# Cross attention of a decoder step: three heads' softmax ahead of the sample rows', outputs and sample sums in the order of their operands, other PSUM banks

## The chip, the cores and the metric

The kernel runs on one core of a Trainium2 chip. The metric is the device time in microseconds (us). Before the change it was 1386.8 us, the median of three runs (1386.02 to 1387.09). An engine's instructions run in an order that is fixed when the program is built; engines wait for one another by semaphores. TensorE (PE) writes its results to eight PSUM banks, ScalarE (ACT) and VectorE (DVE) read them from there.

## The reference

One decoder layer is computed for 256 prompt rows and 8 sample rows, 264 in all, with a model width of 2048. The part that matters here is the cross attention into 256 memory tokens, with four heads of width 128. The prompt rows attend to keys and values computed from the memory; the sample rows attend to keys and values from a cache, a set of their own for each of the 8 rows.

```python
def memory_kv(mem, g_mem, w_ck, w_cv, ck_norm_g):
    h = rms_norm(mem, g_mem)
    k = rms_norm((h @ w_ck).reshape(b, m, MEM_HEADS, MEM_HEAD_DIM), ck_norm_g)
    v = (h @ w_cv).reshape(b, m, MEM_HEADS, MEM_HEAD_DIM)
...
def cross_attend(x, mem_k, mem_v, g_cross, w_cq, cq_norm_g, w_co):
    q = rms_norm((rms_norm(x, g_cross) @ w_cq).reshape(b, t, MEM_HEADS, MEM_HEAD_DIM), cq_norm_g)
    logits = jnp.einsum('bqhd,bshd->bhqs', q, mem_k.astype(q.dtype), ...) * MEM_HEAD_DIM ** -0.5
    p = jax.nn.softmax(logits, axis=-1)
    o = jnp.einsum('bhqs,bshd->bqhd', p.astype(x.dtype), mem_v.astype(x.dtype))
    return o.reshape(b, t, D_XATTN) @ w_co
```

Ahead of it stand an attention and a state-space mixer with their output projection (`w_out`); behind it a feed-forward block (`w_up`, a convolution, a gate, `w_down`).

## The kernel before

The whole layer is one stream of matmuls. Activations lie with features in the partitions and the 264 rows in the free dimension. Every weight is loaded in parts of 128 x 1024 (`weights`, L76), cast to a high part on ScalarE (L89) and a low part on DVE (L90), and each product is three matmuls: high x high, high x low, low x high (`mm3`, L103 to L106). `proj` (L108) runs a projection with its results in PSUM banks and hands them to an evacuation function. The small matrix work, such as logits, transposes and sums, is in full fp32.

PSUM has eight banks, named by tags (L59): `mm` has three, `t` two, and `s`, `x` and `y` one each. A tile of a tag waits until the former tile of the same slot has been read for the last time, in the order in which the program asks for them. So two pieces of work with the same tag cannot overlap where there is one bank.

The order of each engine's instructions is not the program's. A scheduler runs the program in a simulation when it is built: at each step it takes the ready instruction that stands first in the program, and lays down the engine's order that comes out. Program order is thus a priority. `tc.high_priority()` puts instructions ahead (the weight casts and evacuations); `tc.issue_after(x)` makes the instructions of a block stand behind x on x's engine. On the chip the laid-down order stays, whatever the real durations are.

The cross attention runs through these steps. `keys` (L1105) computes the memory keys `kx`. `q_pair` (L1070) computes the queries of two heads; `q_rms` (L1081) their norms `fq`. Then, in program order:

- `sample_probs` (L1134): the sample rows' logits against the cached keys, in two halves of four rows each (L1144, bank `x`), as the `kt` buffers allow; the sum of squares of the sample queries (L1154, bank `y`); the root and its reciprocal (L1158, recorded under the helper's lines L287 and L288); the maximum (L1160); the exponentials (L1163); the normalization (L1165); the transposes (L1168, recorded under L283; bank `t`) and the copies into `pz` (L1172).
- `probs(h, f)` for the four heads (L1194): logits of the prompt rows in bank `s` (L1198), maximum (L1201), two exponentials (L1206), reciprocal and scaling (L1207, L1209), four transposes (L1213, recorded under L283; bank `t`) and a copy into `pts` on ScalarE (L1214). The exponentials lie in a buffer `e` of which there are two.
- `v_pair(0)` (L1217): the memory values of heads 0 and 1 in two of the three banks `mm`, read out by ScalarE (L1230).
- `sample_out` (L1174): the sample rows' output against the cached values (L1180, bank `x`), four steps on DVE that gather each head's columns into `rs` (L1183, L1185), a transpose (L1188, recorded under L283; bank `y`), and the split of the sample columns into high and low parts `OH` and `OL` (recorded under L97).
- `out_head(0)` and `out_head(1)` (L1232): the output of a head for the prompt rows (L1236), in bank `y` for even and `s` for odd heads, and its split (L97).
- `v_pair(1)`, `out_head(2)` and `out_head(3)`.
- the output projection `w_co` (L1289 to L1304) with the residual in `x2_ev` (L1285). Its first weight unit runs through the four heads in turn and needs each head's `OH` and `OL` with the sample columns. The other three stand behind the split of the last head on ScalarE and DVE.

Then the feed-forward block begins: `up(0)` (L1361) takes two banks for each pair of weight units, `mm` for even and `t` for odd ones (L1374). Its results stay in the banks until `r2`, the norm of the rows, is known.

Of the kernel before, what the change touches and what calls it, by code (L numbers as in the profile page):

```python
# [9 lines left out]
AF = mybir.ActivationFunctionType  # L10
ALU = mybir.AluOpType
# [37 lines left out]
def hybrid_decoder_step_kernel(ctx: ExitStack, tc: tile.TileContext, I, O):  # L49
    nc = tc.nc  # L50
    V, S, P, PE = nc.vector, nc.scalar, nc.gpsimd, nc.tensor
# [9 lines left out]
    def psum(tag):  # L61
        return ps.tile([128, 512], F32, tag=tag, name=tag, bufs=banks[tag])
# [38 lines left out]
    marks = {}  # L101
# [47 lines left out]
    op = oc.enter_context(tc.tile_pool(name="op", bufs=1))  # L149
# [135 lines left out]
    def rms(out, ss, n):  # L285

        S.activation(out=out, in_=ss, func=AF.Sqrt, bias=eps[0:out.shape[0]], scale=1.0 / n)  # L287
        V.reciprocal(out=out, in_=out)  # L288
# [141 lines left out]
    p = psum("y")  # L430
# [40 lines left out]
    p = psum("x")  # L471
# [661 lines left out]

    def sample_probs():  # L1134
        lg = psum("x")
        for half in range(2):
            kts = []
            for b in range(4):
                kts.append(wide("kt")[:, 0:1024].rearrange("p (m s) -> p m s", m=4))
                nc.sync.dma_start(out=kts[b], in_=I["mk"][4 * half + b])  # L1140

            def logits(b, m):
                c = 128 * (4 * half + b) + 32 * m
                return PE.matmul(lg[32 * m:32 * m + 32, 0:256], qz[:, c:c + 32], kts[b][:, m, :],  # L1144
                                 start=half == 0 and b == 3, stop=half == 1 and b == 2)

            with tc.issue_after(marks["q"].ins):
                marks["q"] = logits(3, 0)
            with tc.issue_after(marks["q"].ins):
                for b in (3, 0, 1, 2):  # L1150
                    for m in range(b == 3, 4):
                        logits(b, m)
        p = psum("y")
        PE.matmul(p[:, 0:1], qq.rearrange("p m b -> p (m b)"), ones[:, 0:1], start=True, stop=True)  # L1154
        st = xp.tile([128, 4], F32, name="sst")
        fs, mx, den = st[:, 0:1], st[:, 1:2], st[:, 2:3]
        V.tensor_tensor(out=fs, in0=p[:, 0:1], in1=r1s[:, 1:2], op=ALU.mult)
        rms(fs, fs, 128)  # L1158
        V.tensor_tensor(out=fs, in0=fs, in1=r1s[:, 0:1], op=ALU.mult)
        V.tensor_reduce(out=mx, in_=lg[:, 0:256], op=ALU.max, axis=AX.X)  # L1160
# [13 lines left out]
    def sample_out():  # L1174
# [9 lines left out]
        for m in range(1, 4):  # L1184
            V.scalar_tensor_tensor(out=rs, in0=po[:, m * 128:m * 128 + 128], scalar=cst[:, C_M4 + m:C_M4 + m + 1], in1=rs,  # L1185
                                   op0=ALU.mult, op1=ALU.add)
        p = psum("y")
        tr(p[:, 0:128], rs)  # L1188
# [5 lines left out]
    def probs(h, f):  # L1194
        p = psum("s")
        s3 = p.rearrange("p (c k) -> p c k", c=2)
# [7 lines left out]
        e3 = e.rearrange("p (c k) -> p c k", c=2)  # L1204
        for c in range(2):
            S.activation(out=e3[:, c, :], in_=s3[:, c, :], func=AF.Exp, scale=f[:, c:c + 1], bias=mx[:, c:c + 1], accum_out=den[:, c:c + 1])  # L1206
        V.reciprocal(out=den, in_=den)  # L1207
# [55 lines left out]
    OH, OL = OHL[:, 0:4, :], OHL[:, 4:8, :]  # L1263
    sample_probs()
    for b in range(6, 8):
        vts.append(wide("vt")[:, 0:1024].rearrange("p (k n) -> p k n", k=2))
        nc.sync.dma_start(out=vts[b], in_=I["mv"][b])
    for h in range(2):
        probs(h, fq[:, :, h])
    for h in range(2, 4):  # L1270
        probs(h, fq[:, :, h])
    for i in range(2):
        v_pair(i)
        if i == 0:
            sample_out()
        for m in range(2):
            heads = out_head(2 * i + m)
    nc.sync.dma_start(out=O["mem_v"], in_=vx)
# [82 lines left out]
    def up(g):  # L1361
        H = (rows("A", f"hh{g}"), rows("A", f"hl{g}"))
        n = len(groups[g])
        for ii, i in enumerate(groups[g]):
# [8 lines left out]

            proj([w_up[2 * i], w_up[2 * i + 1]], X2, ev, tag="t" if i % 2 else "mm")  # L1374
            cs = []
# [213 lines left out]
```

## Time and profile before

| | |
|---|---|
| Median of three runs | 1386.8 us (1386.02 to 1387.09) |
| The profiled execution | 1386.54 us |
| Its span, first to last instruction | 1384.3 us |
| Granted TensorE clock | 1.000 |
| DVE busy | 1048.7 us (76%) |
| ScalarE busy | 766.1 us (55%) |
| GpSimd busy | 94.8 us (7%) |
| HBM traffic | 215 GB/s over the span |

The profile is of one execution. Its span is 2.2 us less than that execution's own time. Times of single instructions are in microseconds from the span's start; the cross attention's part after the queries lies between 554 and 620. A row of the timeline gives start, duration, engine, line, operation, what is written and read, the shape, how many instructions were merged in the row, and in brackets how long the engine stood idle before it and what ended that. PE's matmuls overlap, so their durations are longer than the distance from one start to the next. A full fp32 matmul has two records. In the row of a window each engine's busy time is given with the number of its instructions; PEld is the loading of weights into PE.

### The profile page before, as it was taken

The numbers are of one execution on the slowest core, as the hardware profiler recorded it, in microseconds if no ns is written. First come the engines' busy times: TensorE is split into PE (matmuls) and PEld (weight loads), VectorE is DVE, ScalarE is ACT, GpSimd is POOL, SyncE is SP. The second block draws the span as 40 slices with busy tenths as digits, with TensorE's granted clock in tenths as the row PEclk, the third lists the DMA queues.
The fourth block names the chain that finished last, engine by engine and source line by source line (L and its number), as shares of the span: only waits on it lengthen the run. The fifth ranks groups of instructions, "written<-read, shape, count | busy, mean of one in ns | idle before, by whom it ended". The sixth has DMA issues, their size and how long they took to land.

```text
span 1384.3 us, 28768 instructions
## 1 busy us (share of the span) xinstructions
PE 1376.5 (99%) x11415; PEld 1348.3 (97%) x11415; DVE 1048.7 (76%) x1865; ACT 766.1 (55%) x1261; POOL 94.8 (7%) x286
## 2 busy tenths in 40 slices
PE   9999999999999999999999999999999999999999
PEld 8999999999999999889999999999999999999998
DVE  7979799999987774478777775777577757765655
ACT  7667755556545555476565544554455445543532
POOL 0000011111000000002010000000000000000000
PEclk9999999999999999999999999999999999999999
DMA  7954467777677566766576765676667656655664
GB/s 296 331 163 135 145 209 254 232 245 259 234 220 239 182 240 211 308 219 193 187 256 216 259 210 188 214 255 214 186 214 244 196 185 198 198 183 185 192 188 139
DMA packets 89477, 298.31 MB, mean 215 GB/s; under 512 B 12032, under 2 KB 17152, under 8 KB 88832
## 3 DMA queue, kind: packets, MB, share of 16 engines
q1 hardware_dynamic: 83840, 277.61, 60.6%
q0 software_dynamic: 5504, 18.88, 4.2%
q8 instruction: 89, 1.46, 0.4%
q14 instruction: 44, 0.36, 0.1%
HBM read 280.77 MB, written 16.23 MB: 215 GB/s over the span
## 4 chain that ended last, share of the span: by engine, by line
PE 97%; DMA 1%; DVE 1%; ACT 0%; issue 0%; SPq 0%; ACTq 0%
PE mm L105 21%; PE mm L104 20%; PE mm L106 20%; PE t L105 10%; PE t L106 9%; PE t L104 9%; PE t L245 1%; PE t L283 1%; PE y L830 1%; DMA wraw<-in_w_co_dram 1%; PE y L846 0%; DMA open<-in_open_dram 0%; PE x L283 0%; DVE wlo L90 0%; PE s L245 0%; PE mm L245 0%
## 5 line engine op out<-in xcount | busy, mean ns | idle before, releaser
L89 ACT CAST whi<-wraw 128x1024 fp32r<-128x1024 f32 x440 | 459.5, 1047 | 518.2 <-PE mm L105 278.3
L90 DVE TENSOR_TENSOR wlo<-wraw,whi 128x1024 fp32r<-128x1024 f32 x440 | 540.7, 1231 | 220.8 <-ACT whi L89 214.9
L105 PE MATMUL t<-x2l,whi 128*128 128x264 f32 x704 | 200.6, 285 | 0.0
L105 PE MATMUL mm<-x2l,whi 128*128 128x264 f32 x704 | 200.5, 285 | 0.0
L105 PE MATMUL mm<-hl,whi 128*128 128x264 f32 x704 | 199.6, 285 | 0.0
L106 PE MATMUL t<-x2h,wlo 128*128 128x264 f32 x704 | 199.1, 283 | 0.0
L106 PE MATMUL mm<-x2h,wlo 128*128 128x264 f32 x704 | 198.7, 283 | 0.0
L106 PE MATMUL mm<-hh,wlo 128*128 128x264 f32 x704 | 197.6, 282 | 0.0
L104 PE MATMUL mm<-x2h,whi 128*128 128x264 f32 x704 | 196.5, 279 | 0.4 <-DVE res L1285 0.4
L104 PE MATMUL t<-x2h,whi 128*128 128x264 f32 x704 | 196.4, 279 | 0.0
L104 PE MATMUL mm<-hh,whi 128*128 128x264 f32 x704 | 194.1, 280 | 0.0
L104 PE MATMUL mm<-xh,whi 128*128 128x264 f32 x576 | 163.8, 286 | 0.0
L105 PE MATMUL mm<-xl,whi 128*128 128x264 f32 x576 | 163.5, 285 | 0.0
L106 PE MATMUL mm<-xh,wlo 128*128 128x264 f32 x576 | 162.1, 286 | 0.0
L104 PEld LDWEIGHTS mm<-x2h,whi 128*128 128x128 f32 x704 | 132.3, 188 | 0.6 <-ACT whi L89 0.6
L104 PEld LDWEIGHTS t<-x2h,whi 128*128 128x128 f32 x704 | 132.3, 188 | 0.0
L106 PEld LDWEIGHTS t<-x2h,wlo 128*128 128x128 f32 x704 | 132.1, 188 | 0.0
L106 PEld LDWEIGHTS mm<-x2h,wlo 128*128 128x128 f32 x704 | 132.1, 188 | 0.0
L106 PEld LDWEIGHTS mm<-hh,wlo 128*128 128x128 f32 x704 | 131.9, 188 | 0.0
L105 PEld LDWEIGHTS mm<-hl,whi 128*128 128x128 f32 x704 | 131.7, 187 | 0.0
L105 PEld LDWEIGHTS mm<-x2l,whi 128*128 128x128 f32 x704 | 131.7, 187 | 0.0
L105 PEld LDWEIGHTS t<-x2l,whi 128*128 128x128 f32 x704 | 131.7, 187 | 0.0
(497 smaller groups left out, 2893.8 us busy)
## 6 DMA issues: line engine op xcount, KB each, us to landing
wraw<-in_w_up_dram SPq DMA_DIRECT2D x176, 512.0 KB, 4.4
wraw<-in_w_in_dram SPq DMA_DIRECT2D x96, 512.0 KB, 4.7
wraw<-in_w_dn_dram SPq DMA_DIRECT2D x88, 512.0 KB, 4.4
wraw<-in_w_out_dram SPq DMA_DIRECT2D x48, 512.0 KB, 4.3
h<-in_h_dram POOLq DMA_DIRECT2D x32, 256.0 KB, 4.6
hn<-in_h_dram SPq DMA_DIRECT2D x16, 512.0 KB, 4.8
out_state_s_dram<-hn POOLq DMA_DIRECT2D x16, 512.0 KB, 3.6
e<-dram_la SPq DMA_DIRECT2D x16, 256.0 KB, 4.8
```

The lines of the kernel that those rows point to most:

```text
L89: S.copy(out=hi, in_=x)
L90: V.tensor_tensor(out=lo, in0=x, in1=hi.bitcast(F32), op=ALU.subtract)
L104: PE.matmul(out, wh, xh, start=start, stop=False)
L105: PE.matmul(out, wh, xl, start=False, stop=False)
L106: return PE.matmul(out, wl, xh, start=False, stop=stop)
L245: PE.matmul(first[c][:, :T], pre[k // 2][i][:, k % 2, c * 128:(c + 1) * 128], A[k // 8][x][:, k % 8, :], start=k + i + x == 0, stop=k == K ...
L283: return PE.transpose(out, in_, cst[0:k, C_ID:C_ID + k])
L830: PE.matmul(y[o:o + 64, (h // 2) * 128:(h // 2) * 128 + 128], xdt[:, h, :], es[h // 4][:, h % 4, :], start=True, stop=True)
```

## The change

The sample rows' logits, their norm and their softmax, one function so far, become three. The root is remembered in `marks["root"]`, and the exponentials of the prompt rows' heads stand behind it on ScalarE. In program order the softmax of heads 0, 1 and 2 is named ahead of the sample rows', that of head 3 behind it. The logits of heads 1 and 3 use bank `y`, those of 0 and 2 bank `s`. The outputs of heads 0 and 1 are named ahead of `sample_out`, whose transposed sums go to bank `x`. The first pair of `up` units takes banks `s` and `x`; the later ones are as before.

```diff
-    def sample_probs():
+    def sample_logits():
         lg = psum("x")
...
+        return lg
+
+    def sample_scale():
         p = psum("y")
         PE.matmul(p[:, 0:1], qq.rearrange("p m b -> p (m b)"), ones[:, 0:1], start=True, stop=True)
         st = xp.tile([128, 4], F32, name="sst")
+        fs = st[:, 0:1]
+        V.tensor_tensor(out=fs, in0=p[:, 0:1], in1=r1s[:, 1:2], op=ALU.mult)
+        marks["root"] = S.activation(out=fs, in_=fs, func=AF.Sqrt, bias=eps, scale=1.0 / 128)
+        V.reciprocal(out=fs, in_=fs)
+        V.tensor_tensor(out=fs, in0=fs, in1=r1s[:, 0:1], op=ALU.mult)
+        return st
+
+    def sample_probs(lg, st):
         fs, mx, den = st[:, 0:1], st[:, 1:2], st[:, 2:3]
-        V.tensor_tensor(out=fs, in0=p[:, 0:1], in1=r1s[:, 1:2], op=ALU.mult)
-        rms(fs, fs, 128)
-        V.tensor_tensor(out=fs, in0=fs, in1=r1s[:, 0:1], op=ALU.mult)
...
-        p = psum("y")
+        p = psum("x")
         tr(p[:, 0:128], rs)
...
     def probs(h, f):
-        p = psum("s")
+        p = psum("y" if h % 2 else "s")
...
-        for c in range(2):
-            S.activation(out=e3[:, c, :], in_=s3[:, c, :], func=AF.Exp, ...)
+        with tc.issue_after(marks["root"].ins):
+            for c in range(2):
+                S.activation(out=e3[:, c, :], in_=s3[:, c, :], func=AF.Exp, ...)
...
-    sample_probs()
+    lg = sample_logits()
+    sst = sample_scale()
     for b in range(6, 8):
         vts.append(wide("vt")[:, 0:1024].rearrange("p (k n) -> p k n", k=2))
         nc.sync.dma_start(out=vts[b], in_=I["mv"][b])
-    for h in range(2):
+    for h in range(3):
         probs(h, fq[:, :, h])
-    for h in range(2, 4):
-        probs(h, fq[:, :, h])
+    sample_probs(lg, sst)
+    probs(3, fq[:, :, 3])
     for i in range(2):
         v_pair(i)
+        for m in range(2):
+            heads = out_head(2 * i + m)
         if i == 0:
             sample_out()
-        for m in range(2):
-            heads = out_head(2 * i + m)
...
-            proj([w_up[2 * i], w_up[2 * i + 1]], X2, ev, tag="t" if i % 2 else "mm")
+            proj([w_up[2 * i], w_up[2 * i + 1]], X2, ev, tag=["s", "x"] if i == 0 else "t" if i % 2 else "mm")
```

More of the change, by code (lines that the diff above doesn't have):

```diff
@@ L1204, in probs @@
         e3 = e.rearrange("p (c k) -> p c k", c=2)
-        for c in range(2):
-            S.activation(out=e3[:, c, :], in_=s3[:, c, :], func=AF.Exp, scale=f[:, c:c + 1], bias=mx[:, c:c + 1], accum_out=den[:, c:c + 1])
+        with tc.issue_after(marks["root"].ins):
+            for c in range(2):
+                S.activation(out=e3[:, c, :], in_=s3[:, c, :], func=AF.Exp, scale=f[:, c:c + 1], bias=mx[:, c:c + 1], accum_out=den[:, c:c + 1])
         V.reciprocal(out=den, in_=den)
```

## The prediction

> **What bounds the kernel now.** I read the page first, for its engine sums and for the chain that ended last.
>
> ```profile
> PE 1376.5 (99%) x11415; PEld 1348.3 (97%) x11415; DVE 1048.7 (76%) x1865; ACT 766.1 (55%) x1261; POOL 94.8 (7%) x286
> ...
> PE 97%; DMA 1%; DVE 1%; ACT 0%; issue 0%; SPq 0%; ACTq 0%
> ```
>
> TensorE (PE) is busy for 1376.5 of 1384.3 us and holds 97% of the chain. DVE, with 76%, has room. So a change of order, which alters no matmul's size, can gain only what PE now loses by standing still; and it loses what it newly makes PE wait for. The next view is therefore the waits, PE alone, over the whole execution:
>
> ```profile
> PE x L206 <- DVE eps L279: 1.2, 1, 1.2
> PE s L1198 <- ACT ohl L97: 1.0, 1, 1.0
> PE s L1236 <- ACT e L1206: 0.9, 1, 0.9
> PE y L283 <- DVE rs L1185: 0.6, 1, 0.6
> PE mm L104 <- DVE res L1285: 0.4, 1, 0.4
> PE t L245 <- ACT whi L188: 0.3, 1, 0.3
> ```
>
> The first and last row belong to the opening. The four between them are all in the part that is changed: logits of a head (L1198) waiting for ScalarE, the output matmuls of a head (L1236) waiting for a head's exponentials (L1206), the transpose of the sample sums (L283) waiting for DVE, and the first up-projection matmul (L104) waiting for the evacuation of a bank (L1285). Together they are 2.9 us. The ends of matmuls are modelled in this trace, so I also measured from start to start, in PE's timeline. The columns are start, duration, line, operands, count, idle time before it.
>
> ```profile
> 587.29 0.60 PE L283 MATMUL t<-cst,e 128*128 128x128 f32 x4
> 588.50 0.33 PE L283 MATMUL y<-cst,rs 128*128 128x128 f32 x1 [0.60 <-DVE rs L1185]
> 589.80 1.13 PE L1198 MATMUL s<-qk 128*128 128x256 f32 x4 [0.97 <-ACT ohl L97]
> ...
> 591.21 1.03 PE L1236 MATMUL y<-vp 128*128 128x256 f32 x4
> 593.15 1.13 PE L1236 MATMUL s<-vp 128*128 128x256 f32 x4 [0.92 <-ACT e L1206]
> ...
> ```
>
> ```profile
> 619.10 0.28 PE L105 MATMUL mm<-ohl,whi 128*128 128x264 f32 x1
> 619.22 0.28 PE L106 MATMUL mm<-ohl,wlo 128*128 128x264 f32 x1
> 619.91 0.36 PE L104 MATMUL mm<-x2h,whi 128*128 128x264 f32 x1 [0.40 <-DVE res L1285]
> ```
>
> The time that PE really needs for such groups comes from the chain of waits, whose pieces end where the next one starts:
>
> ```profile
> 581.05 0.86 PE s L1198 x4
> ...
> 582.83 3.62 PE x L1180 x32
> ...
> 590.93 0.45 PE t L283 x4
> ...
> 595.09 0.86 PE y L1236 x4
> ```
>
> Four transposes take 0.45 us, so 0.11 each; a head's logits 0.86 (they count as four records); a head's output 0.86; the sample rows' output matmuls 3.62. A projection matmul takes 0.12 (619.10 to 619.22).
>
> **The change part by part.** Head by head the arithmetic is unchanged: same matmuls, same activations, same bytes, same number of DMAs. What changes is who stands before whom, and in which PSUM bank.
>
> *Second bank for the logits.* Before, heads 0 to 3 share bank s, so each head's logits wait until the former head's two exponentials have read it. The transpose of the sample sums starts at 588.50 and needs 0.11; the logits of head 3 start at 589.80: lost 1.19. With heads 1 and 3 in y the reader to wait for is the one two heads back. The same bank s is used by the output of head 1, behind head 3's exponentials: head 0's output starts at 591.21 and needs 0.86, head 1's starts at 593.15: lost 1.08.
>
> *Softmax of three heads ahead.* This part decides whether those waits reappear elsewhere. ScalarE now:
>
> ```profile
> 566.58 0.30 ACT L287 ACTIVATE sst<-sst,eps 128x1 f32<-128x1 f32 x1 [0.28 <-DVE sst L1157]
> ...
> 567.86 0.47 ACT L1230 ACTIVATE vp<-mm,rmc 128x256 f32<-128x256 f32 x1 [0.98 <-PE mm L106]
> ...
> 576.80 1.28 ACT L1163 ACT_TABLE_LOAD   x1 [1.98 <-DVE sst L1161]
> 578.10 0.56 ACT L1163 ACTIVATE es<-x,sst 128x256 f32<-128x256 f32 x1
> 578.65 0.56 ACT L1206 ACTIVATE e<-s,st,fq 128x256 f32<-128x256 f32 x1
> ...
> 579.19 0.56 ACT L1206 ACTIVATE e<-s,st,fq 128x256 f32<-128x256 f32 x1
> ...
> 583.38 0.58 ACT L1206 ACTIVATE e<-s,st,fq 128x256 f32<-128x256 f32 x1
> ...
> 588.55 0.56 ACT L1206 ACTIVATE e<-s,st,fq 128x256 f32<-128x256 f32 x1
> ...
> 591.90 0.56 ACT L1206 ACTIVATE e<-s,st,fq 128x256 f32<-128x256 f32 x1
> ```
>
> The root of the sample rows' norm is the row at 566.58; the exponential table is loaded at 576.80, after 1.98 us of waiting for the sample rows' maximum, and no head's exponentials run before that. So ScalarE leaves 566.88 to 576.80 without any softmax, and all four heads fall behind the end of the value matmuls:
>
> ```profile
> 582.22 0.28 PE L106 MATMUL mm<-whi,ml 128*128 128x256 f32 x1
> ```
>
> After this last value matmul PE has only small work left, which waits on DVE and ScalarE. In the new order the load comes right behind the root: 566.88 + 1.28 = 568.16, then the two exponentials of head 0 (0.54 apart, 578.65 to 579.19) until 569.3. Before, one head's exponentials follow the former's by 583.38 − 578.65 = 4.73, 5.17 and 3.35 us on one bank; with two banks that spacing is a ceiling for every second head. So head 2 comes no later than 568.2 + 5.2 = 573.4, and three heads are through before 576.80. The sample rows' exponentials need their logits, which come no earlier than now, so they run at 576.80 in place of 578.10: the load is no longer in front of them. Head 3 follows at about 578. That there is room on the two engines is shown by the stretch concerned (columns: PE, PEld, DVE, ACT, POOL busy):
>
> ```profile
> 566.00:580.00 14.00, 14.00 (x139) 12.95 (x138) 6.44 (x12) 7.54 (x14) 0.00 (x0) 1.00 0.85 326
> ```
>
> DVE works for 6.44 and ScalarE for 7.54 of 14 us. ScalarE gets the load and six exponentials at 0.56, 4.6 us, for 6.5 that are free; DVE has 7.6 free.
>
> *What is queued behind.* On ScalarE the copies of the first value pair (567.86) now stand behind the load and up to four exponentials, till about 570.4, 2.5 us later. They free the matmul bank that one half of the second value pair waits for. The other half sits in the third bank: 48 matmuls at 0.12 are 5.8 us of cover, so I cost this at nothing; without that cover it is 2.5. The weight casts are marked urgent, and PE has no wait for one after the opening; nothing.
>
> *Outputs of heads 0 and 1 ahead of the sample sums; the transposed sums in x.* Bank x is free when their own operand is, so it costs nothing, and y is left to the heads. The lost time goes if the sample chain ends under other work. Now: four transposes of head 1 end at 587.29 + 0.45 = 587.74, the transpose of the sums starts at 588.50: lost 0.76. This chain is
>
> ```profile
> 586.47 0.35 DVE L1183 TENSOR_SCALAR rs<-x,cst 128x128 f32<-128x128 f32 x1 [1.02 <-PE x L1180]
> ...
> 590.52 0.17 DVE L97 TENSOR_TENSOR ohl<-y,ohl 128x16 fp32r<-128x16 f32 x1
> ```
>
> with 4.5 us from the last sample matmul (582.83 + 3.62 = 586.45, less the rounding of the pieces 0.2) to the second split at 590.69. In the new order PE does, before the value matmuls end, also two heads' logits (1.72), three heads' transposes (1.35), two outputs (1.72) and the sample output (3.62), so their end moves from 582.34 to at most 590.8. The sample output started 4.73 after its exponentials (578.10 to 582.83); from 576.80 this gives 581.5, its end 585.2, the split done at 589.7, 1.1 us before the value matmuls end. So it lies under them. Behind their end come the value copies (0.47 each) and the outputs of heads 2 and 3, under 24 matmuls of the output projection for heads 0 and 1 (2.9 us).
>
> *Banks s and x for the first up-projection.* The first matmul would start at 619.22 + 0.12 = 619.34 but starts at 619.91, when DVE has emptied a bank mm: 0.57. Banks s and x are long empty by then. Next late would be the weights; PE has no wait for them anywhere in the waits view. Gain 0.57.
>
> *Sum.* 1.19 + 1.08 + 0.76 + 0.57 = 3.60 us at most, 2.9 by the waits view. Against it stand about ten new places where a small PE step meets DVE or ScalarE inside the matmul stream (logits and transposes of four heads, the sample transposes and output). The trace shows no price for them in the new order; it lies between nothing, if the value matmuls cover all, and the mean of the four old waits, 0.9, for each. I take 0.4 for all together, near the lower end, by these rows of two small steps that already stand in that stream:
>
> ```profile
> 559.75 0.41 DVE L1094 COPY raw<-y 128x256 f32<-128x256 f32 x1
> ...
> 578.98 0.35 DVE L1165 TENSOR_SCALAR es<-es,sst 128x256 f32<-128x256 f32 x1
> ```
>
> ```profile
> 562.21 0.38 PE L283 MATMUL y<-cst,raw 128*128 128x128 f32 x2
> ```
>
> ```profile
> 580.43 0.38 PE L283 MATMUL t<-cst,es 128*128 128x128 f32 x2
> ```
>
> The copy at 559.75 is done at 560.16 and its transposes come at 562.21; the scaling at 578.98 is done at 579.33 and its transposes come at 580.43. The written-out order puts such steps 1 to 2 us behind their operand, so the chip does not wait. The net gain is 3.2 us. The profiled execution took 1386.54 (2.2 around its span); that gives 1383.3, and, as it stands 0.26 under the median of the runs, 1383.6 in the median.
>
> **The rivals.**
>
> *The table load in a place that counts.* It now precedes three heads. If the order of PE was laid out without it, the transposes of head 0 come 1.28 us late once, with value matmuls queued behind: 1383.6 + 1.3 = 1384.9. For it: nothing on PE depended on that load so closely before. Against it: the lead of 1 to 2 us above. What a load costs behind other work is shown by a second one:
>
> ```profile
> 634.47 1.05 ACT L89 CAST whi<-wraw 128x1024 fp32r<-128x1024 f32 x1 [1.83 <-PE t L105]
> 635.54 1.28 ACT L287 ACT_TABLE_LOAD   x1
> 636.83 0.48 ACT L287 ACTIVATE r<-y,eps 128x264 f32<-128x264 f32 x1
> ```
>
> Cast, load and root follow each other within 0.03 us, so 1.28 is all. [...]
>
> *The sample rows come last.* If their output matmuls are placed behind the value matmuls, the 4.5 us chain to their split is covered by the outputs of heads 2 and 3 alone (1.72), since every matmul of the output projection reads the sample columns too: 2.8 of the 3.6 come back, 1386.0. It decides if the sample output starts later than about 586, 4.5 later than I reckon. For it: DVE and ScalarE now serve head 2 and 3 next to the sample rows. Against it: the load is gone from that chain.
>
> *New waits in the stream: slower.* PE's instructions run in the order written out for it. A logits group or a transpose that is placed too early holds up the value matmuls behind it, where before it held up nothing but its like. At 0.9 each, four such places eat the gain of 3.6; seven of the ten cost 6.3, net 2.7 slower, 1389.5. Against it: the lead shown above, and PE's list of waits, which has no entry within the value matmuls, where such steps stand already.
>
> *The order does not take effect.* Program order is a priority only; if the heads stay where they are, only the bank for the up-projection counts: 1386.2. Against it: the maximum and the exponentials of the heads have nothing else to wait for.
>
> **How the numbers follow.** A measurement of this kernel tells about 0.2%, 2.8 us, from no change; the forecast, 3.2, is little more than that, so its chance is split. Forecast 0.52, of which 0.48 is faster by over 2.8 and 0.04 falls short of it. The table load 0.14 (0.02 faster, 0.12 same). The sample rows last 0.15, same. No effect 0.06, same. New waits 0.13 (0.11 slower, 0.02 same). This gives faster 0.50, same 0.39, slower 0.11. The low end is the whole 3.6 and half of the runs' spread (1.07): 1382.7. The high end takes in every case but the new waits: 1386.8.
>
> **What would show it.** The profile after would have: a load of the exponential table near 567 and none near 577; exponentials of three heads before the sample rows'; no PE wait for L1206 or for the sample sums; PE's first up-projection matmul 0.12 after the last output-projection matmul. The forecast is wrong if PE's waits name a head's transposes, logits or outputs between 566 and 600, if value matmuls stand still behind the copies of the first value pair, or if the sample sums are transposed after the last value matmul.

## The result, and the profile after

The changed kernel took 1382.93 us in the median of eight runs (1382.12 to 1383.25), the kernel before 1386.73 us in eight runs beside them (1385.74 to 1387.12). The ratio is 0.9975, with a 95% interval from 0.9965 to 0.9984: 3.8 us faster, the forecast being 1383.6. The profiled execution of the changed kernel took 1382.65 us, with a span of 1380.6.

The page of the changed kernel, engine sums and chain:

```profile
PE 1375.4 (100%) x11415; PEld 1348.0 (98%) x11415; DVE 1050.0 (76%) x1865; ACT 765.8 (55%) x1261; POOL 96.1 (7%) x286
...
PE 99%; DMA 0%; ACT 0%; SPq 0%; DVE 0%; issue 0%
```

PE's busy time is 1.1 us less and its span 3.7 us less; most of what went is time between its instructions. The waits of PE in the changed kernel, the whole list:

```profile
PE x L206 <- DVE eps L279: 1.2, 1, 1.2
PE t L245 <- ACT whi L188: 0.5, 1, 0.5
```

Both belong to the opening. The four waits of the cross attention are gone. (The line numbers of the changed kernel are eight to ten higher than before: L1198, the logits, is L1206 now; the heads' exponentials L1206 are L1215; the outputs L1236 are L1245; the sample rows' exponentials L1163 are L1171; the evacuation L1285 is L1295.)

Since the opening varies from execution to execution, I measure the changed part by itself: from the start of the first value matmul to the start of the first down-projection matmul, both read in PE's timeline. Before: 554.13 to 804.77, 250.64 us. Changed: 553.86 to 801.02, 247.16 us. The part has gained 3.48 us. What lies behind it lasts 579.5 us in both; the rest of the difference of the two profiled executions, 0.27 us, lies ahead of the part and isn't the change's. The part is read from one execution of each kernel. It can be trusted to a few hundredths where the granted clock stays at 1.00: the kernel before and "up banks alone" below differ only in the banks of the first up pair, and their times for the value matmuls, logits, transposes, sample output, sums and outputs, taken as in the table below, agree to 0.01 us.

ScalarE's timeline in the changed kernel (columns as in the prediction):

```profile
566.32 0.29 ACT L1161 ACTIVATE sst<-sst,eps 128x1 f32<-128x1 f32 x1 [0.28 <-DVE sst L1160]
566.63 1.28 ACT L1215 ACT_TABLE_LOAD   x1
567.93 0.56 ACT L1215 ACTIVATE e<-s,st,fq 128x256 f32<-128x256 f32 x1
...
569.03 0.47 ACT L1239 ACTIVATE vp<-mm,rmc 128x256 f32<-128x256 f32 x1
...
572.58 0.56 ACT L1215 ACTIVATE e<-y,st,fq 128x256 f32<-128x256 f32 x1 [1.78 <-DVE st L1210]
...
574.15 0.58 ACT L1215 ACTIVATE e<-s,st,fq 128x256 f32<-128x256 f32 x1
...
578.12 0.57 ACT L1171 ACTIVATE es<-x,sst 128x256 f32<-128x256 f32 x1 [1.17 <-DVE sst L1169]
...
579.15 0.58 ACT L1215 ACTIVATE e<-y,st,fq 128x256 f32<-128x256 f32 x1
```

The load stands right behind the root, three heads run ahead of the sample rows, head 3 behind them. Head 1 waits 1.78 us and the sample rows 1.17 us for their maximum on DVE. DVE's timeline shows why:

```profile
570.46 1.23 DVE L90 TENSOR_TENSOR wlo<-wraw,whi 128x1024 fp32r<-128x1024 f32 x1 [0.48 <-ACT whi L89]
571.60 0.68 DVE L1209 TENSOR_REDUCE st<-y 128x2 f32<-128x512 f32 x1
...
576.33 1.23 DVE L90 TENSOR_TENSOR wlo<-wraw,whi 128x1024 fp32r<-128x1024 f32 x1
577.47 0.42 DVE L1168 TENSOR_REDUCE sst<-x 128x1 f32<-128x256 f32 x1
```

Each time the low part of a weight, 1.23 us, stands ahead of the maximum. PE's timeline of the place where the sample chain meets the heads' outputs:

```profile
584.26 2.34 PE L1188 MATMUL x<-va,pz 128*32 128x512 f32 x18
...
590.89 0.28 PE L106 MATMUL mm<-whi,ml 128*128 128x256 f32 x1
591.01 0.27 PE L283 MATMUL x<-cst,rs 128*128 128x128 f32 x1
...
593.02 0.59 PE L104 MATMUL mm<-ohl,whi 128*128 128x264 f32 x2
```

And DVE's at the same place:

```profile
588.36 1.13 DVE L1193 SCALAR_TENSOR_TENSOR rs<-x,cst,rs 128x128 f32<-128x128 f32 x3
...
592.20 0.17 DVE L97 TENSOR_TENSOR ohl<-x,ohl 128x16 fp32r<-128x16 f32 x1 [0.24 <-ACT ohl L97]
```

The sample sums are complete at 589.49, but their transpose was laid behind the last value matmul, at 591.01. Their split ends at 592.37, and PE's first matmul that reads the sample columns starts at 593.02, after the outputs of heads 2 and 3: 0.65 us to spare.

The next table adds up, for kinds of matmuls in the part, the time from each start to the next start on PE; a wait is thereby charged to the matmul ahead of it. The last two columns are experiments, below.

| PE, us | before | changed | two logits banks alone | one logits bank, casts held behind |
|---|---|---|---|---|
| value matmuls | 22.94 | 24.05 | 23.13 | 23.65 |
| logits of the heads | 2.61 | 2.03 | 2.51 | 2.22 |
| transposes of the heads | 2.44 | 1.39 | 2.73 | 1.77 |
| sample output | 3.57 | 3.57 | 3.57 | 5.65 |
| transposed sample sums | 1.30 | 0.37 | 0.66 | 1.37 |
| outputs of the heads | 4.08 | 3.18 | 3.88 | 3.57 |
| output projection, to the first up matmul | 24.27 | 23.23 | 23.43 | 23.14 |
| all else | 189.43 | 189.34 | 189.35 | 189.35 |
| the part | 250.64 | 247.16 | 249.26 | 250.72 |

By these rows the small steps and the output projection lost 4.5 us, and the value matmuls, with more small steps among them, became 1.11 us dearer. But most of that 1.11 is the way of charging. A value matmul that follows a small step starts just behind the step's last record, and the gap behind it is longer in return. Head 1's logits in PE's timeline of the changed kernel:

```profile
568.42 1.03 PE L1206 MATMUL y<-qk 128*128 128x256 f32 x4
569.09 0.47 PE L104 MATMUL mm<-whi,mh 128*128 128x256 f32 x1
569.40 0.28 PE L105 MATMUL mm<-wlo,mh 128*128 128x256 f32 x1
```

From 568.42 to 569.40 it is 0.98 us: 0.12 for the one value matmul and 0.86 for the logits, the price that the prediction gives for a head's logits among small steps. The table charges 0.31 (569.09 to 569.40) to the value matmul. If the projection matmul behind a small step of the heads or of the sample output is charged its usual 0.11 or 0.12 and the rest goes to the step, the value matmuls take 22.66 before and 22.72 in the changed kernel, and small steps and output projection together lose 3.45: transposes of the heads 0.77, transposed sums 0.93, outputs 1.08, output projection with the first up matmul 0.58, logits 0.20; the sample output costs 0.11 more. So the new places cost next to nothing.

### The profile page after: what moved, and what is told of

Same layout as the page of the kernel before. It is cut to its first block, busy times and chain, and to the rows that moved or that the text cites. A ratio compares the mean times of both kernels' runs of the same rounds, so it can differ in the third digit from the quotient of the medians.

```text
span 1380.6 us, 28767 instructions
## 1 busy us (share of the span) xinstructions
PE 1375.4 (100%) x11415; PEld 1348.0 (98%) x11415; DVE 1050.0 (76%) x1865; ACT 765.8 (55%) x1261; POOL 96.1 (7%) x286
## 4 chain that ended last, share of the span: by engine, by line
PE 99%; DMA 0%; ACT 0%; SPq 0%; DVE 0%; issue 0%
PE mm L106 21%; PE mm L104 21%; PE mm L105 21%; PE t L106 10%; PE t L104 10%; PE t L105 10%; PE t L245 1%; PE t L283 1%; PE y L830 1%; PE y L846 0%; PE x L283 0%; DMA open<-in_open_dram 0%; PE s L245 0%; PE mm L245 0%; PE t L564 0%; PE x L1144 0%
## 5 line engine op out<-in xcount | busy, mean ns | idle before, releaser
L104 PE MATMUL mm<-x2h,whi 128*128 128x264 f32 x672 | 189.3, 282 | 0.0
L105 PE MATMUL mm<-x2l,whi 128*128 128x264 f32 x672 | 189.3, 282 | 0.0
L106 PE MATMUL mm<-x2h,wlo 128*128 128x264 f32 x672 | 189.3, 282 | 0.0
L104 PEld LDWEIGHTS mm<-hh,whi 128*128 128x128 f32 x704 | 130.8, 187 | 0.0
L104 PEld LDWEIGHTS mm<-x2h,whi 128*128 128x128 f32 x672 | 125.9, 187 | 0.0
L105 PEld LDWEIGHTS mm<-x2l,whi 128*128 128x128 f32 x672 | 125.9, 187 | 0.0
```

Source lines behind the costliest of these rows:

```text
L104: PE.matmul(out, wh, xh, start=start, stop=False)
L105: PE.matmul(out, wh, xl, start=False, stop=False)
L106: return PE.matmul(out, wl, xh, start=False, stop=stop)
```

## The experiments

My theory: the edits remove four waits, each by its own means. The rivals: one of the edits does it all; the early exponentials cost or give nothing; or the gain hangs on their being made together. Each kernel ran beside the kernel before on the same chip. "The part" is the stretch defined above, from the profiled execution. The part and the medians tell the same within 0.4 us in every row but that of "own buffer for es", and where a ratio's interval takes in 1, the reading rests on the part alone.

| kernel | the part, us | less 250.64 | median, us | kernel before | ratio (95%) |
|---|---|---|---|---|---|
| first up pair back in mm | 556.77 to 804.39, 247.62 | -3.02 | 1383.18 | 1386.40 | 0.9981 (0.9971 to 0.9990) |
| up banks alone | 553.35 to 803.33, 249.98 | -0.66 | 1385.51 | 1386.40 | 0.9994 (0.9984 to 1.0003) |
| one logits bank | 554.78 to 809.92, 255.14 | +4.50 | 1391.29 | 1386.40 | 1.0036 (1.0023 to 1.0049) |
| sample rows first | 553.54 to 801.81, 248.27 | -2.37 | 1384.02 | 1386.40 | 0.9983 (0.9974 to 0.9993) |
| no hold behind the root | 554.82 to 804.01, 249.19 | -1.45 | 1384.93 | 1386.27 | 0.9990 (0.9981 to 1.0000) |
| sums first, in y | 554.07 to 804.18, 250.11 | -0.53 | 1385.75 | 1386.27 | 0.9999 (0.9990 to 1.0008) |
| four heads ahead | 553.89 to 806.90, 253.01 | +2.37 | 1388.88 | 1386.27 | 1.0018 (1.0009 to 1.0027) |
| own buffer for es | 554.49 to 809.82, 255.33 | +4.69 | 1389.64 | 1386.27 | 1.0028 (1.0016 to 1.0039) |
| four ahead, casts held behind | 554.20 to 802.79, 248.59 | -2.05 | 1383.85 | 1386.10 | 0.9983 (0.9974 to 0.9993) |
| one bank, casts held behind | 553.37 to 804.09, 250.72 | +0.08 | 1386.45 | 1386.10 | 1.0005 (0.9995 to 1.0015) |
| two logits banks alone | 554.02 to 803.28, 249.26 | -1.38 | 1385.03 | 1386.10 | 0.9992 (0.9983 to 1.0002) |
| sums in y | 553.81 to 800.99, 247.18 | -3.46 | 1382.63 | 1386.10 | 0.9975 (0.9965 to 0.9984) |

**First up pair back in mm**, the changed kernel with one line undone:

```diff
-            proj([w_up[2 * i], w_up[2 * i + 1]], X2, ev, tag=["s", "x"] if i == 0 else "t" if i % 2 else "mm")
+            proj([w_up[2 * i], w_up[2 * i + 1]], X2, ev, tag="t" if i % 2 else "mm")
```

> The kernel after, with the first pair of up-projection units back in the banks mm. All figures are of the profile; the stretch is the distance from the start of the first value matmul to the start of the first down-projection matmul, 250.64 us before and 247.16 after. Theory (the gain is the sum of the four waits of PE that went): the wait of L104 for DVE's evacuation comes back with its 0.57, stretch 247.7, time about 1383.5; the three waits of the softmax part stay away. Rival (the bank is worth nothing now, since DVE starts its evacuations earlier): stretch 247.2, no wait, 1382.9.

The wait for L1295 is back in the list of PE's waits, with 0.2 us. By the starts it is 0.50 from the last output-projection matmul to the first up matmul (619.04 to 619.54) in place of 0.12, and the part is 0.46 longer.

**Up banks alone**, the same line put into the kernel before.

> The kernel before, with only the banks s and x for the first pair of up-projection units. Theory (four separate waits): the three waits of the softmax part stay with 3.03, the fourth goes, stretch 250.64 - 0.57 = 250.07, time about 1386.2. Rival (DVE is the engine behind this point, and PE waits for its weights or rows in place of the bank): stretch 250.6, a PE wait for L90 or L99, 1386.7.

The part is 0.66 shorter and the three other waits stay, at 1.0, 0.9 and 0.6. This edit stands for itself, at 0.5 to 0.7 us in both surroundings.

**Sample rows first**: the changed kernel, but the sample rows' softmax named ahead of the four heads'.

```diff
-    for h in range(3):
-        probs(h, fq[:, :, h])
     sample_probs(lg, sst)
-    probs(3, fq[:, :, 3])
+    for h in range(4):
+        probs(h, fq[:, :, h])
```

> The kernel after, with the sample rows' softmax named first and then the four heads, as before; second bank, outputs ahead of sample sums and other banks stay. Theory (the heads' early place carries the gain): the heads' exponentials fall behind the sample rows' again, near 578, and waits on PE come back for one or more heads; stretch 249 to 250, time 1384.8 to 1385.8. Rival (the banks carry it): stretch 247.2 to 247.7, time about 1383.2.

The table load is back at its old place, and two small waits of PE come up. ScalarE's timeline, then the waits:

```profile
577.29 1.28 ACT L1171 ACT_TABLE_LOAD   x1
```

```profile
PE y L1245 <- ACT e L1215: 0.4, 1, 0.4
PE s L1245 <- ACT vp L1223: 0.2, 1, 0.2
```

The part is 1.11 us longer than in the changed kernel: between the two theories, nearer to the rival. The early softmax, which I took for the part that decides whether the waits reappear, is worth a third of the gain.

**No hold behind the root**: the changed kernel without the hold that keeps the heads' exponentials behind the sample rows' root.

```diff
-        with tc.issue_after(marks["root"].ins):
-            for c in range(2):
-                S.activation(...)
+        for c in range(2):
+            S.activation(...)
```

> The kernel after, without the order that keeps the heads' exponentials behind the root. Head 0's exponentials then stand ahead of the root, with a load of the exponential table before them, one of the root's table before the root, and one of the exponential table after it: two loads more, 2.57 us at 1.28 each. The stretch from the first value matmul to the first down-projection matmul is 250.64 us before and 247.16 after. Theory (ScalarE has cover under the value matmuls): no new wait on PE, stretch 247.2, time about 1382.9. Rival (the load counts, as in the prediction's first rival): PE waits for a head's or the sample rows' step, stretch 248.4 to 249.7, time 1384.2 to 1385.5.

Head 0's exponentials slip in ahead of the root, and the table is loaded three times. ScalarE's timeline, then the wait of PE:

```profile
567.02 1.28 ACT L1214 ACT_TABLE_LOAD   x1
...
569.53 1.28 ACT L1161 ACT_TABLE_LOAD   x1
...
575.02 1.28 ACT L1214 ACT_TABLE_LOAD   x1 [2.23 <-DVE st L1210]
576.32 0.56 ACT L1214 ACTIVATE e<-y,st,fq 128x256 f32<-128x256 f32 x1
```

```profile
PE t L283 <- DVE e L1217: 2.0, 1, 2.0
```

Head 1's exponentials start at 576.32, 21.50 us after the part's start, in place of 572.58, 18.72 after: 2.8 us later. The third load, between the maximum and them, is 1.28 of that. The second one does it by a detour: the weight cast behind it on ScalarE starts at 571.39, its low part runs on DVE at 572.45, and head 1's maximum stands behind that at 573.60; counted from the part's start each is 1.0 later than in the changed kernel. The 0.5 that are left are the maximum of head 2, which DVE takes here ahead of the step that follows head 1's maximum (L1210, at 574.79). PE stands 2.0 us at a transpose, and the part is 2.03 us longer. So the rival of the prediction, a table load in a place that counts, exists; the hold is what keeps it away.

**One logits bank**: the changed kernel with all heads' logits in s.

```diff
-        p = psum("y" if h % 2 else "s")
+        p = psum("s")
```

> The kernel after, with the logits of all four heads in bank s again; the order of the program stays. Theory of the prediction (the second bank takes away 1.19 + 1.08): a wait for a head's exponentials comes back on PE, stretch 248.5 to 249.4, time 1384.3 to 1385.2. Rival (being early under the value matmuls is enough, since a late head then holds up nothing): no wait for L1215 on PE, stretch at most 247.5, time about 1383.2.

Both theories missed: 7.98 us longer than the changed kernel, 4.50 longer than the one before. **Four heads ahead**, the changed kernel with `range(4)` in place of `range(3)` and head 3's own line gone, missed in the same way:

> The kernel after, with all four heads named ahead of the sample rows' softmax. Theory (the sample chain is the one with the least slack: in the kernel after its last split ended 0.65 us before the first output-projection matmul): head 3's exponentials (1.1 us) ahead of the sample rows' use up that slack, and a wait of up to 0.5 to 1 us comes at the first output-projection matmul; stretch 247.5 to 248.2, time 1383.3 to 1384. Rival (three or four is indifferent): no wait, stretch 247.2, 1382.9.

Both have one new wait of the same length. In "four heads ahead" PE's timeline shows it, and the windows show what follows it (columns: PE, PEld, DVE, ACT, POOL busy, granted clock, DMA share, GB/s):

```profile
597.44 0.81 PE L104 MATMUL mm<-ohl,whi 128*128 128x264 f32 x2 [3.98 <-ACT ohl L97]
...
600.46 0.42 PE L104 MATMUL mm<-ohl,whi 128*128 128x264 f32 x1
600.68 0.35 PE L105 MATMUL mm<-ohl,whi 128*128 128x264 f32 x1
```

```profile
594.00:597.40 3.40, 0.00 (x0) 0.00 (x0) 2.66 (x4) 1.89 (x4) 0.00 (x0) 1.00 0.84 267
597.40:600.80 3.40, 3.36 (x15) 3.36 (x16) 0.17 (x1) 0.00 (x0) 0.00 (x0) 0.50 0.99 339
```

PE waits for the sample columns from 593.5 on. When it starts again its clock is granted at 0.50 for 3.4 us: matmuls are 0.22 apart (600.46 to 600.68), where they are 0.12 apart from 600.88 on. In 3.4 us at half the clock 1.7 us of work are done, so that costs another 1.7. 4.0 and 1.7 are 5.7 of the 5.85 us that this kernel takes more than the changed one. What keeps the sample columns away stands in ScalarE's timeline:

```profile
593.38 0.37 ACT L97 CAST ohl<-s 128x256 fp32r<-128x256 f32 x1
593.65 1.99 ACT L89 CAST whi<-wraw 128x1024 fp32r<-128x1024 f32 x2
595.55 0.17 ACT L97 CAST ohl<-x 128x16 fp32r<-128x16 f32 x1
597.22 0.17 ACT L97 CAST ohl<-x 128x16 fp32r<-128x16 f32 x1 [1.50 <-DVE ohl L97]
```

The later weights of the output projection are held until the last head's output is split, and then they are urgent. Where the outputs of the last heads come ahead of the sample sums, that split lets two weights go, 1.99 us on ScalarE and 2.36 us on DVE, and the 0.17 us casts of the sample columns stand behind them. In the changed kernel the order is the other way round.

The sample output started 2.1 us later here than in the changed kernel (586.35, 584.26). So it could be that lateness, and not the weights. **Four ahead, casts held behind** tells the two apart: the later weights are also held behind the sample columns' split.

```diff
-            split(OH[:, :, cs], OL[:, :, cs], x)
+            marks["sums"] = split(OH[:, :, cs], OL[:, :, cs], x)
...
-        with tc.issue_after(heads[0].ins), tc.issue_after(heads[1].ins):
+        with tc.issue_after(heads[0].ins), tc.issue_after(heads[1].ins), tc.issue_after(marks["sums"][0].ins), tc.issue_after(marks["sums"][1].ins):
```

> Edit: the changed kernel with all four heads' softmax ahead of the sample rows', and in addition the casts of the output projection's later weights are held behind the split of the sample columns. Theory (the 4.0 us wait of the version without this hold comes from the weight casts that stand ahead of the sample columns' casts on ScalarE and DVE, and the half clock that follows comes from that wait): the casts of the sample columns now follow the outputs' casts at once, the wait shrinks to 1.0 to 1.6 us, no half clock follows, and the stretch from the first value matmul to the first down-projection matmul falls from 253.01 to 248.2 to 249.2. Rival (the late sample exponentials and the place of the sample output make the loss; the casts only happen to stand there): the stretch stays at 251.5 to 253, with a wait of over 2.5 us or several of them.

ScalarE's timeline, then PE's:

```profile
593.70 0.37 ACT L97 CAST ohl<-s 128x256 fp32r<-128x256 f32 x1
593.97 0.18 ACT L97 CAST ohl<-x 128x16 fp32r<-128x16 f32 x1
...
594.71 2.00 ACT L89 CAST whi<-wraw 128x1024 fp32r<-128x1024 f32 x2
```

```profile
594.87 0.51 PE L104 MATMUL mm<-ohl,whi 128*128 128x264 f32 x2 [1.10 <-ACT ohl L97]
```

The wait is 1.10 us in place of 3.98, the clock stays at 1.00, and the part is 4.42 us shorter, as expected. So the weight casts are shown to be the cause of the cliff. With them out of the way the fourth head's place still costs 1.43 us (248.59 less 247.16), of which 1.10 is the wait that is left.

**One bank, casts held behind** does the same for the version with one logits bank.

> Edit: the changed kernel with all logits back in bank s, and the casts of the output projection's later weights held behind the split of the sample columns. Theory (two losses in the one-bank version: the same wait of 4.0 us with its half clock, and a bank cost of its own): the wait shrinks to 1.0 to 1.6 us without a half clock, the stretch falls from 255.14 to 250.3 to 251.3, and what is left over the changed kernel's 247.16, 3 to 4 us, is the price of the single bank with its order. Rival (the single bank alone keeps the sample chain late): over 252.5.

250.72, as expected. The wait is 1.1 us here too. Where the other loss lies is in the table above: the sample output takes 5.65 us in place of 3.57. PE's timeline:

```profile
585.52 1.92 PE L1188 MATMUL x<-va,pz 128*32 128x512 f32 x16
587.37 1.13 PE L1245 MATMUL s<-vp 128*128 128x256 f32 x4
588.43 1.04 PE L1188 MATMUL x<-va,pz 128*32 128x512 f32 x2
589.41 0.33 PE L283 MATMUL t<-cst,e 128*128 128x128 f32 x1
```

With one bank for the logits the heads' steps come late and are laid in between the sample output's matmuls. Sixteen of these in a row take 1.85 us (585.52 to 587.37), two that stand apart 0.98 (588.43 to 589.41). In the row they start four at a time, within 0.02 us, and the next four 0.41 to 0.43 later; each of the two that stand apart is followed after 0.45 or 0.52, so one alone takes as long as four. With the early softmax but one bank, nothing at all is left of the gain.

**Two logits banks alone**: the kernel before with only the heads' banks changed.

```diff
-        p = psum("s")
+        p = psum("y" if h % 2 else "s")
```

> Edit: the kernel before with one word changed: heads 1 and 3 put their logits in bank y; order of naming, sums and up-projection as before. Theory (prediction's sum: the logits' wait of 1.19 and the output's wait of 1.08 are the bank's): stretch 250.64 less up to 2.3, so 248.3 to 249.2, with the waits for the sample sums and for the up-projection's bank left. Rival (bank y is also the sample sums' and the outputs', so a third user there returns what it saves; in addition the last output's cast falls behind two weight casts, as in the versions that lost): 250.3 or more, with a new PE wait for a split of an output.

249.26, 1.38 us less than before and just outside the theory's 248.3 to 249.2; my sum for this edit was 1.19 + 1.08. The two waits that it was to remove are off the list, but four small ones stand in the part, 1.4 us together; the largest, 0.46, is the transpose of the sample sums, which waits for bank y until a head's exponentials have read it. And of the 1.38 us, 0.57 is not that edit's aim at all: the first up matmul follows the last one of the output projection by 0.12 (618.38 to 618.50), because the order there came out otherwise.

**Sums first, in y**: the changed kernel with `sample_out` named ahead of heads 0 and 1 and the transposed sums in y, as it was before.

```diff
-        p = psum("x")
+        p = psum("y")
         tr(p[:, 0:128], rs)
...
+        if i == 0:
+            sample_out()
         for m in range(2):
             heads = out_head(2 * i + m)
-        if i == 0:
-            sample_out()
```

> The kernel after, with the sample rows' output and sums named ahead of the outputs of heads 0 and 1 and the transposed sums in bank y again, both as before. Theory: the output of head 0, which uses bank y too, falls behind the sums' split; the chain of the sums then has less work to lie under, and PE waits for the sums or for head 0's bank, 0.5 to 1.5 us; stretch 247.7 to 248.7, time 1383.4 to 1384.4. Rival (all of it lies under the value matmuls, the order of the two is indifferent): stretch 247.2, time about 1382.9.

250.11, beyond what I expected; 2.95 us of the gain are lost. PE's waits:

```profile
PE mm L104 <- ACT ohl L97: 1.5, 1, 1.5
PE y L1245 <- DVE ohl L97: 0.6, 1, 0.6
```

Bank y goes round in the order of naming, so the output of head 0 has to wait until the late sample sums have been read: it starts at 591.87. Behind it the cliff shows again in small: ScalarE casts two of the later weights from 592.17 on, 1.99 us, ahead of the cast of head 0's output at 594.06, and PE's 1.5 us are a wait for that cast. **Sums in y** separates naming and bank: the outputs are named first, as in the changed kernel, and the sums are in y.

> Edit: the changed kernel with one word changed: the transposed sample sums go in bank y again, outputs still named ahead of them. (Named in the other order, with bank x kept, the instruction lists of all engines are those of the changed kernel, so the bank is the only question.) Theory (bank x is needed because y would hold the outputs of heads 0 and 2 back until both sample splits have read it, and two weight casts then stand ahead of the last output's cast): 0.5 to 1.5 us more than the changed kernel, 247.7 to 248.7, as a wait at the first output-projection matmuls or the outputs in y. Rival (the outputs in y are covered by the output-projection matmuls placed ahead of them): 247.0 to 247.4, no new PE wait. Second rival (the same cliff as the version with the sums ahead of the outputs): 250 or more.

247.18, the changed kernel's time: the first rival holds. With bank x, on the other hand, both orders of naming give the same instruction lists. So either of the two edits is enough, and only the lack of both costs 2.95.

**Own buffer for es** asks what held the heads' exponentials behind the sample rows' in the kernel before, where by my prediction nothing did. Of the kernel before, only the sample rows' exponentials are given another buffer.

```diff
-        e = xp.tile([128, 512], F32, tag="e", name="es", bufs=2)[:, 0:256]
+        e = small.tile([128, T], F32, tag="sq", name="es")[:, 0:256]
```

> The kernel before, with one edit: the sample rows' exponentials are written to another buffer than the two of the heads. In the kernel before ScalarE ran no head's exponentials between 567 and 577 although head 0's operands were ready at 565. Theory (the heads were held back by the queue for the shared buffers, not by their rank in the program): the heads' exponentials move ahead of the sample rows' without any change of the program's order, and part of the gain comes; one bank and the old order of outputs and sums stay, so waits of 1 to 2.5 remain: stretch 248.5 to 250, time 1384.6 to 1386.1. Rival (rank): the order stays, stretch 250.6, 1386.7.

The heads move ahead at once (ScalarE's timeline):

```profile
566.69 1.28 ACT L1206 ACT_TABLE_LOAD   x1
567.98 0.57 ACT L1206 ACTIVATE e<-s,st,fq 128x256 f32<-128x256 f32 x1
...
569.21 1.28 ACT L287 ACT_TABLE_LOAD   x1
...
574.23 1.28 ACT L1206 ACT_TABLE_LOAD   x1 [1.76 <-DVE st L1202]
```

So it was the pair of `e` buffers. They are given out in the order of naming; in the kernel before no head got one until the sample rows' exponentials had theirs, and head 0's follow these at once (578.10 and 578.65 in the prediction's rows). But the part is 4.69 us longer than before, not shorter, and the median 3.37. The execution that was profiled took 1391.63, 2.0 more than the median of its kernel. On one logits bank the sample output is broken into pieces (5.51 us in place of 3.57), PE waits 1.76 us at the first output-projection matmul and in several smaller places. This version has no hold behind the root either, and so it loads the table three times, as the version without the hold does; what of the loss is the bank's and what the loads', no run separates. And the clock drops (windows):

```profile
596.68:600.09 3.41, 1.00 (x7) 0.75 (x6) 2.75 (x4) 1.76 (x3) 0.00 (x0) 1.00 0.94 332
600.09:603.50 3.41, 3.41 (x12) 3.05 (x13) 0.42 (x1) 0.37 (x1) 0.00 (x0) 0.50 1.03 420
```

## Why the prediction was right, and which of its steps were not

The time, the sign and the four waits came out as forecast. Point by point:

- *Sum.* 3.60 gross less 0.4 was forecast, 3.48 net was measured in the part. With the charging put right (below the table) the four terms came out one by one: 1.08 for 1.08 at the outputs, 0.77 for 0.76 at the transposes ahead of the sums, 0.58 for 0.57 at the up-projection, and 0.93 for 1.19 at the sums. The 0.26 that are missing there are still in the changed kernel: behind the transposed sums PE starts the next output at 591.38, not at 591.12, while ScalarE copies the second value pair (590.85 to 591.69). The term that was mis-sized is the 0.4 for the ten new places: against the 3.60 stand 0.12 in all, and by the corrected rows the value matmuls paid 0.06.
- *Medians.* 1386.73 less 1382.93 is 3.80; 0.3 more than the part gives, about the 0.27 by which the two profiled executions differ ahead of it. In the version with the up pair back in mm the part begins at 556.77, 2.9 later than in the changed kernel, with nothing changed ahead of it: the opening differs by that much between two executions. PE's timeline of that version shows why:

```profile
8.64 0.42 PE L245 MATMUL mm<-xh,whi 128*128 128x264 f32 x1
8.86 0.42 PE L245 MATMUL s<-xh,whi 128*128 128x264 f32 x1
```

Up to 10.80 us its matmuls start 0.22 apart, the same distance as at the granted 0.50 above; in the changed kernel they are 0.12 apart from 5.20 on (42 matmuls between 5.20 and 10.80, against 24 in this version). If the clock was at half there, 5.6 us of it are 2.8 us of work: an estimate from these distances, since the granted clock in the windows view reads 1.00 in both. (In the changed kernel the trace's record of it begins at 5.20 and in the one before at 6.36, where the distance falls from 0.22 to 0.12.)

- *Second bank for the logits: 1.19 + 1.08.* Right as waits that went, wrong as the price of one edit. Alone it gives 1.38, of which 0.57 is elsewhere; taken out, it costs 7.98, or 3.56 without the weights' cliff. The waits had not one cause each: when the bank is free, the next late thing is the head's own exponentials.
- *Softmax ahead.* The load ran at 566.63 (forecast 566.88), head 0 right behind it. "Head 2 no later than 573.4" failed by 0.75: it ran at 574.15. The ceiling was taken from the bank alone, and the maximum of head 1 stood behind a low part of a weight on DVE. For the same reason the sample exponentials ran at 578.12, not at 576.80. DVE's 7.6 free us were there, but not where they were needed; a busy share says nothing about who stands ahead of whom.
- *Copies of the first value pair.* They came 1.2 us later (567.86 to 569.03), not 2.5, since two exponentials stood ahead of them, not four. No wait of PE came of it, as forecast.
- *Sample chain under the value matmuls.* Failed by place. "The split done at 589.7, 1.1 us before the value matmuls end" became 592.37, 1.5 after them (590.89). The sample output started at 584.26, not 581.5: 1.3 us from the later exponentials, 1.4 because it stood 6.1 behind them in PE's order, not 4.7. From its end (584.26 + 3.57) to the split it is 4.5 us, as forecast, though 1.5 of these are the transpose's place behind the value matmuls. Sums that are transposed after the last value matmul are on the prediction's own list of signs that it is wrong; the sign came, and no wait came with it. The time was kept by the cover that the prediction gave to heads 2 and 3, with 0.65 us to spare. That much is luck: the prediction had 1.1 us of room ahead of the value matmuls' end, and with four heads ahead, 2.1 us later, the room was gone.
- *Bank x for the sums.* "Costs nothing" was right; that it is needed was not: y with the outputs named first takes the same time.
- *Banks s and x for the up-projection: 0.57.* Right: 0.46 and 0.66.
- *Rivals.* The table load in a place that counts: shown by the version without the hold, at 2.0 us. In the changed kernel the load follows the root by 0.02 us (566.32 + 0.29 to 566.63) and the exponentials the load by 0.02. At the three loads of the version without the hold the next instruction starts 0.01 to 0.02 behind the load. The sample rows last: "it decides if the sample output starts later than about 586". It started at 584.26, and the version with four heads ahead, 2 us later, is just beyond that point. There the price is 5.85, not 2.8: I had not seen the weights that pass by the sample columns, nor the clock. Without the weights it is 1.43. New waits in the stream: none came; PE's list has no entry within the value matmuls. The order takes no effect: its argument against itself, that "the maximum and the exponentials of the heads have nothing else to wait for", was wrong. In the kernel before they waited for an `e` buffer; moving the naming lifts that.

What stays open is what the early softmax is worth put alone into the kernel before, with its hold behind the root: it was only taken out of the changed kernel (1.11 us), or brought about by other means with three table loads (own buffer for es).

## What to carry to other kernels

The waits of one stretch could be added up here (3.60 forecast, 3.48 gained), but not shared out among the edits: two edits alone gave 0.66 and 1.38 us, and undoing one of them made the kernel slower than before. A table of distances from start to start charges a change of kind to the matmul behind it (above, 0.31 us to a value matmul that takes 0.12); look two starts on before calling a row dearer. When small steps are moved, look at what their end releases: two urgent weight casts, 2 us together, that got in front of a 0.17 us cast cost 4.42 us, more than the 3.48 that the change gained. Buffers and banks that are shared go round in the order of naming, so a late step that is named first holds an early one; change the naming, or give one of them a place of its own.

## What the runs showed of the hardware

Behind 3.98 us of waiting PE's clock was granted at 0.50 for 3.4 us (four heads ahead, 597.40 to 600.80), an estimated 1.7 us on top. Behind a wait of the same length in the version with one logits bank it was 0.50 from 600.80 to 604.00 and 1.00 from there on. Behind a wait of 1.10 us it stayed at 1.00 (four ahead, casts held behind). It also fell in the version with the own buffer for es, to 0.50 from 600.09 to 603.50, where PE's longest wait in the part was 1.76 us; PE had worked for 1.00 us of the 3.41 before the drop. In the version with the sums first, in y, it worked for 1.27 of 3.40 us (593.00 to 596.40) and the clock stayed at 1.00. What decides whether a stop costs the clock, these runs do not show.

The clock differed between executions of one kernel. Of the seven runs of the own buffer for es, two with a mean granted clock of 1.000 took 1389.29 and 1389.49 us, two with 0.999 took 1389.44 and 1389.64, and three with 0.998 took 1391.03 to 1392.62. Only one of them, with 0.998, left a trace.

The sample output's matmuls (tiles of 128*32) take 0.12 us each in a row (1.85 for 16) and 0.49 each in twos between others (0.98 for two). Cutting their run into pieces cost 2.08 us (5.65 in place of 3.57; one bank, casts held behind) without a wait on any list.
